# Dilated attention with V as weights: outputs feature by token, shares spread by 0/1 products, halves of y_b inside the attention groups

## The chip, the cores and the metric

One core of a Trainium2 chip runs the whole layer. The metric is the device time of one execution in microseconds (us). Five engines run in parallel, each through its own queue in program order: PE (TensorE: weight loads and matmuls), DVE (VectorE), ACT (ScalarE), POOL (GpSimd) and SP, which here issues most DMA transfers. A matmul keeps one operand, the weights, in the array and streams the other, the moving operand, through it.

## What is computed

A decoder layer on x of 2048 tokens by 1024 features, all in float32:

```python
proj = x @ w_in[l] + b_in[l]
q, k, v, g_attn, u_lru, g_lru, gate_logits = jnp.split(proj, SPLIT_POINTS, axis=-1)
...
for g, (window, dilation) in enumerate(DILATION_GROUPS):   # (128,1), (512,4), (2048,16)
    o_g, lse_g = dilated_band_attention(q[:, :, g], k[:, :, g], v[:, :, g], window, dilation)
wts = jax.nn.softmax(jnp.stack(lses, axis=0), axis=0)
attn = jnp.sum(wts[..., None] * jnp.stack(outs, axis=0), axis=0)
attn = attn.reshape(B, S, ATTN_OUT_WIDTH).astype(dt) * jax.nn.silu(g_attn)
y_a = attn @ w_attn_proj[l]
...
y_b = (h * jax.nn.silu(g_lru)) @ w_lru_proj[l]
merged = gates[:, :, 0] * y_a + gates[:, :, 1] * y_b
out = merged @ w_out[l] + b_out[l]
x = layer_norm(DEEPNORM_ALPHA * x + out, ln_gain[l], ln_bias[l])
```

Each of the three groups has 8 heads of 64 features. In a group, the tokens of one residue modulo the dilation form a sequence, cut into blocks of 128 queries; a block sees its own 128 keys and, where there is one, the block before.

## The kernel before

The kernel runs in four stretches. **Stage A** (to about 1456 us of the trace) is the input projection: 72 feature tiles by 4 token chunks of 512, by one Strassen step, with every product as three fp32r products of split halves (high by high, high by low, low by high); rotary q and k, V, the LRU branch and the gates hang on it and end in DRAM scratch. Its order is a list of ticks with due times and a budget per engine. **Stage B** (1456 to 1720 us) is attention. **Stage C** (1720 to 1905 us) is y_b = (gated h) times w_lru_proj, with the combination of the three groups beside it. **Stage D** (from 1905 us) is y_a, the merge, w_out and the layer norm.

Stage B goes over 12 units; a unit is a pair of heads of one group (order of the groups: 0, 2, 1, four times), with 16 query blocks; step `j` handles two blocks. `scores(j)` gives for both heads of the pair q times k: the heads lie in partitions 0 to 63 and 64 to 127, so that a product has 64 rows, and the two heads' products stand next to each other in the queue and go to different PSUM banks. q and k are split in halves (`q_split`, `k_split` on ACT and POOL), three products a head. Group 2 has no block before; there 256 columns are computed all the same and half of them not used. `weigh(m)` adds the mask and takes the minimum (the negated maximum) in one DVE operation, then ACT takes exp; the minimum lies beside the outputs in tile `osb`. `turn_p(j)` turns the shares p by transposes, in halves of 64 queries (64 rows each, banks t0 and t1); `copy_p` brings them to `ptb` in SBUF. `values(j)` takes `ptb` as weights (128 keys by 128 queries) and streams V with a column of ones, 65 columns a head, in plain float32; DVE copies the result to `osb`, and POOL issues the store to `o_scr`. Steps are interleaved by hand: two steps of scores, turns of earlier ones, then the values of two steps, so that four blocks make one round.

Stage C has 32 jobs of 24 products (`yb_job`: chunk c, feature tile f; 128 rows, 512 columns, fp32r), the weights `WL` split once for all chunks. `combine` loads three groups' outputs token by feature, takes exp of the differences of the minima, scales on POOL by a broadcast, adds, turns the result by four transposes (`ctp`) and gates it into `at_scr`.

Of the kernel before, what the change touches and what calls it, by code (L numbers as in the profile page):

```python
# [8 lines left out]
F32 = mybir.dt.float32  # L9
# [22 lines left out]
def hybrid_block_kernel(ctx: ExitStack, tc: tile.TileContext, a: dict, out: bass.AP):  # L32
# [10 lines left out]
    o_scr = [[dram.tile([S, 132], F32, name=f"o_scr{g}{hp}") for hp in range(HP)] for g in range(3)]  # L43
# [28 lines left out]
    bn = cst.tile([P, 72], F32, name="bn")  # L72
    lr = cst.tile([P, 8, 8], F32, name="lr")
# [23 lines left out]
    X = ctx.enter_context(tc.tile_pool(name="X", bufs=1))  # L97

    def big(slot, shape, dt, name):
        return (Y if slot[0] == "Y" else Z if slot[0] == "Z" else X).tile(shape, dt, name=name, tag=slot)  # L100

# [40 lines left out]
    LAST_SLOTS = [*range(15, 19), *range(29, 32), *range(28, 18, -1), *range(14, -1, -1)]  # L142
# [254 lines left out]
    def silu_chain(y, sgn, f, c):  # L397
# [3 lines left out]
        act.activation(y, y, AF.Identity, scale=0.5 * sgn, bias=bh[:, f:f + 1])  # L401
# [370 lines left out]
    QSLOT, KSLOT = ("X3", "X1", "Y0"), ("X4", "Y3")  # L772
    VSLOT = {(0, 0): "X5", (2, 0): "Y1", (1, 0): "Y2", (0, 1): "X5", (2, 1): "Y1", (1, 1): "Y2"}
    KR = {}

    units = {}
# [5 lines left out]
    def k_parts(u):  # L782

        g, hp = unit(u)
        src = qk_scr["k", 4 * g + hp].rearrange("(d h) s -> h d s", h=2)

        def part(h, hs):
            def fn():
                if h == 0 and u % 2 == 0:
                    KR["t"] = big(("X2", "X0")[u // 2 % 2], [P, 2, S], F32R, f"C{u}")  # L790
                if h == 0:
                    units[u] = [None, None, KR["t"][:, u % 2]]
                sp.dma_start(flat(units[u][2][hs]), src[h])
            return fn

        return [part(0, lo_), part(1, up_)]

    def k_split(u, x):

        if x == 0:  # L800
            units[u][1] = big(KSLOT[u % 2], [P, S], F32R, f"B{u}")

        def piece(t):
            if unit(u)[0] == 2:
                return t.rearrange("p (c x) -> p c x", c=4)[:, :, 256 * x:256 * x + 256]
            return t[:, 1024 * x:1024 * x + 1024]

        lo, hi = piece(units[u][2]), piece(units[u][1])
        pool.tensor_copy(hi, flat(lo))
        pool.tensor_tensor(out=lo, in0=flat(lo), in1=flat(hi), op=ALU.subtract)  # L810

    def q_parts(u):

        g, hp = unit(u)
        q = qk_scr["q", 4 * g + hp].rearrange("(d h) s -> h d s", h=2)

        def part(h):
            def fn():
                if h == 0:
                    units[u][0] = big(QSLOT[u % 3], [P, 2, S], F32R, f"A{u}")  # L820
                sp.dma_start(flat(units[u][0][(lo_, up_)[h], 1]), q[h])
            return fn

        return [part(h) for h in range(2)]

    def q_split(u, i):

        hi, lo = (units[u][0][:, x, i * CH:(i + 1) * CH] for x in range(2))
        act.activation(hi, flat(lo), AF.Copy)
        pool.tensor_tensor(out=lo, in0=flat(lo), in1=flat(hi), op=ALU.subtract)  # L830

    VT = {}

    def v_parts(g, j):
        src = v_scr[g][j]

        def part(i):
            def fn():
                if i == 0:
                    VT[g, j] = big(VSLOT[g, j], [P, 16, 260], F32, f"V{g}{j}")  # L840
                V = VT[g, j]
                if g == 0:
                    sp.dma_start(V[:, 4 * i:4 * i + 4], src[i * CH:(i + 1) * CH].rearrange("(n p) f -> p n f", p=P))
                elif g == 1:
                    sp.dma_start(V[:, 4 * i:4 * i + 4], src[i * CH:(i + 1) * CH].rearrange("(j r) f -> j r f", r=4))
                else:
                    sp.dma_start(V[:, 4 * i:4 * i + 4], src.rearrange("(i r) f -> i r f", r=16)[:, 4 * i:4 * i + 4])
            return fn

        return [part(i) for i in range(4)]  # L850


    def biases():
        dve.tensor_scalar(out=bh, in0=b72, scalar1=0.5, scalar2=None, op0=ALU.mult)
        dve.tensor_scalar(out=bn, in0=b72, scalar1=-1.0, scalar2=None, op0=ALU.mult)

# [45 lines left out]
    firstv = v_parts(0, 0)  # L902
    R0 = {}

    def first_raw(n):
        for i in K4:
            r = R0[n, i] = take(f"r{n}{i}", F32)
            src = qk_scr[n, 0].rearrange("(d h) s -> h d s", h=2)
            for h, hs in enumerate((lo_, up_)):
                sp.dma_start(r[hs], src[h][:, i * CH:(i + 1) * CH])  # L910

    def first_tiles():
        KR["t"] = big("X2", [P, 2, S], F32R, "C0")
        units[0] = [None, None, KR["t"][:, 0]]

    def first_split(n, i):
        if n == "q" and i == 0:
            units[0][0] = big(QSLOT[0], [P, 2, S], F32R, "A0")
        if n == "k" and i == 0:
            units[0][1] = big(KSLOT[0], [P, S], F32R, "B0")  # L920
        A, B, C = units[0]
        cs = slice(i * CH, (i + 1) * CH)
# [12 lines left out]
    for T, (s, j) in enumerate(where):  # L935
# [10 lines left out]
        if s == NQ - 1:  # L946
            for fn in begin.get(j, ()):
                fn()
            for x in split0.get(j, ()):
                first_split(*x)  # L950
# [585 lines left out]
```

## Time and profile before

| | |
|---|---|
| time, median of 3 runs | 2181.79 us (2179.45 to 2183.22) |
| the profiled execution | 2181.37 us; span of its trace 2179.5 us |
| stage A, 0 to 1456 us | PE busy 1449.9 us |
| stage B, 1456 to 1720 us | PE busy 260.0, DVE 193.5, ACT 221.9, POOL 169.1 us |
| stage C, 1720 to 1905 us | PE busy 183.0, DVE 144.1, ACT 33.6, POOL 99.0 us |
| stage D, 1905 to 2179.5 us | PE busy 262.3, DVE 188.1, ACT 34.9, POOL 46.5 us |
| granted TensorE clock | 0.999 of full speed |

Busy time of PE is the union of its matmuls, each from its start to its modelled end; since one starts long before the one ahead has ended, a busy PE says that work stood in the array, not how fast it went. What one matmul costs in a stream is read from a run of them: the run's length by their number. A product in plain float32 stands twice in the trace (600 `values` products in the program, 1200 matmuls in the trace); an fp32r product and a transpose stand once.

### The profile page before, as it was taken

How to read it: one execution, taken by the hardware profiler on the slowest of the kernel's cores; microseconds unless marked ns; L12 is line 12 of the kernel's file. 1: busy time of each engine (PE TensorE's matmuls, PEld its weight loads, DVE VectorE, ACT ScalarE, POOL GpSimd, SP SyncE). 2: the span in 40 equal slices, each digit the busy share in tenths (PEclk: the TensorE clock that was granted, in tenths of full speed). 3: DMA queues.
4: the chain of work that ended last, by engine and by line, in shares of the span. 5: the costliest groups of instructions: out<-in, count | busy, mean ns of one | idle time of the engine just before them, and what ended most of it. 6: DMA issues, size and time to landing. Idle time of an engine off the chain costs nothing.

```text
span 2179.5 us, 35322 instructions
## 1 busy us (share of the span) xinstructions
PE 2155.2 (99%) x12025; PEld 1803.7 (83%) x12025; DVE 1703.7 (78%) x3209; ACT 1220.3 (56%) x2206; POOL 774.1 (36%) x603
## 2 busy tenths in 40 slices
PE   9999999999999999999999999999999999999998
PEld 7888888888888888888888888879999878888786
DVE  8787987998899767687688798667777588867667
ACT  5456456557556666767767877758888511221100
POOL 2544554555555011021021021027666356622120
PEclk9999999999999999999999999999999999999999
DMA  7876976977877775676575675698774688864431
GB/s 227 255 220 195 264 228 204 265 224 235 256 216 230 242 221 172 184 220 175 184 221 165 198 230 176 189 292 242 208 196 130 191 282 281 263 203 149 156 116 68
DMA packets 257187, 456.05 MB, mean 209 GB/s; under 512 B 58752, under 2 KB 89504, under 8 KB 254192
## 3 DMA queue, kind: packets, MB, share of 16 engines
q1 hardware_dynamic: 237984, 412.70, 60.4%
q0 software_dynamic: 14128, 32.19, 7.1%
q10 hardware_dynamic: 4896, 8.92, 1.1%
q8 instruction: 95, 1.56, 0.3%
q14 instruction: 84, 0.69, 0.1%
HBM read 290.07 MB, written 163.64 MB: 208 GB/s over the span
## 4 chain that ended last, share of the span: by engine, by line
PE 55%; DMA 4%; issue 4%; DVE 2%; ACT 1%; POOL 1%; SPq 0%; ACTq 0%; POOLq 0%; DVEq 0%
PE q L627 32%; PE o L1063 5%; PE yb L1301 2%; PE yb L1299 2%; PE yb L1300 2%; PE s L1003 2%; PE pt L1032 2%; DMA V<-v_scr 1%; PE z L1413 1%; PE z L1412 1%; PE z L1411 1%; POOL me L1382 1%; PE g L488 1%; DMA atr<-at_scr 1%; ACT p L1018 1%
## 5 line engine op out<-in xcount | busy, mean ns | idle before, releaser
L627 PE MATMUL q<-xT,hS 128*128 128x512 f32 x1632 | 504.7, 390 | 0.0
L627 PE MATMUL q<-xT,l 128*128 128x512 f32 x1088 | 423.7, 389 | 0.1
L627 PE MATMUL q<-xB,hA 128*128 128x512 f32 x1344 | 417.4, 392 | 0.0
L627 PE MATMUL q<-xB,l 128*128 128x512 f32 x944 | 367.8, 390 | 1.7 <-DMA l<-wl_scr 1.7
L627 PEld LDWEIGHTS q<-xT,hS 128*128 128x128 f32 x1632 | 304.8, 188 | 64.3 <-issue 1.8
L627 PEld LDWEIGHTS q<-xB,hA 128*128 128x128 f32 x1344 | 250.4, 188 | 56.6 <-issue 5.5
L627 PEld LDWEIGHTS q<-xT,l 128*128 128x128 f32 x1088 | 204.2, 188 | 43.3 <-DMA l<-wl_scr 0.5
L233 POOL TENSOR_TENSOR sw<-sw,sin 128x512 f32<-128x512 f32 x96 | 155.8, 1628 | 167.8 <-ACT sw L322 71.3
L627 PEld LDWEIGHTS q<-xB,l 128*128 128x128 f32 x944 | 177.3, 188 | 39.4 <-DMA l<-wl_scr 2.1
L233 POOL TENSOR_TENSOR y<-y,h 128x512 f32<-128x512 f32 x28 | 39.2, 1399 | 384.1 <-DVE h L529 368.0
L627 PE MATMUL q<-xB,hS 128*128 128x512 f32 x544 | 168.8, 391 | 1.1 <-DVE v L233 1.1
L627 PE MATMUL q<-xT,hA 128*128 128x512 f32 x544 | 167.9, 390 | 0.0
L277 ACT ACTIVATE hA<-wA 128x512 fp32r<-128x512 f32 x220 | 138.6, 636 | 31.8 <-DVE l L233 11.6
L1018 ACT ACTIVATE p<-p,osb 128x256 f32<-128x256 f32 (+1 forms) x384 | 145.3, 451 | 18.9 <-DVE osb L1016 18.3
L277 ACT ACTIVATE hS<-S 128x512 fp32r<-128x512 f32 x170 | 108.4, 638 | 64.4 <-DVE S L233 46.1
L1063 PE MATMUL o<-V,ptb 128*128 128x65 f32 x1200 | 144.4, 277 | 0.0
L1063 PEld LDWEIGHTS o<-V,ptb 128*128 128x128 f32 x1200 | 137.7, 192 | 3.3
L233 POOL TENSOR_TENSOR l<-wA,hA 128x512 fp32r<-128x512 f32 x68 | 110.3, 1622 | 84.7 <-ACT hA L277 51.2
L1016 DVE CUSTOM_DVE_ANT_0 p<-s,mask 128x256 f32<-128x256 f32 (+1 forms) x384 | 116.9, 361 | 24.2 <-PE s L1003 16.9
L627 PEld LDWEIGHTS q<-xB,hS 128*128 128x128 f32 x544 | 101.2, 188 | 22.6 <-issue 2.2
L627 PEld LDWEIGHTS q<-xT,hA 128*128 128x128 f32 x544 | 101.8, 188 | 21.8 <-ACT hA L277 0.4
L233 DVE TENSOR_TENSOR S<-S,wA 128x512 f32<-128x512 f32 x102 | 98.2, 963 | 11.6 <-DMA wA<-in_w_in_dram 8.1
(207 smaller groups left out, 4645.8 us busy)
## 6 DMA issues: line engine op xcount, KB each, us to landing
wA<-in_w_in_dram SPq DMA_DIRECT2D x220, 256.0 KB, 5.1
wl_scr<-l SPq DMA_DIRECT2D x102, 512.0 KB, 5.3
l<-wl_scr SPq DMA_DIRECT2D x102, 512.0 KB, 4.4
wS<-in_w_in_dram SPq DMA_DIRECT2D x102, 256.0 KB, 4.3
wS<-in_w_in_dram POOLq DMA_DIRECT2D x68, 256.0 KB, 6.9
mg_scr<-y SPq DMA_DIRECT2D x59, 256.0 KB, 5.1
o_scr<-osb POOLq DMA_DIRECT2D x48, 264.0 KB, 5.4
oc<-o_scr SPq DMA_DIRECT2D x48, 264.0 KB, 4.9
```

Source lines behind the costliest of these rows:

```text
L233: eng.tensor_tensor(out=out, in0=in0, in1=in1, op=op)
L277: act.activation(heads(h), heads(r, False), AF.Copy)
L488: pe.matmul(g, gw[hs, l], x[hs], start=(n == 0), stop=(n == 2))
L627: pe.matmul(bank, w[:, ks], x[:, kk, xx], start=(first and i == 0), stop=(last and i == 11))
L1003: pe.matmul(bank[h][:, b, (0 if g == 2 and n else lo):256], A[hs, x, n * P:(n + 1) * P], k, start=(i == 0), stop=(i == 2))
L1016: dve.tensor_tensor_reduce(out=p[:, h, lo:256], in0=bank[h][:, m % 2, lo:256], in1=mask[:, lo:256], scale=1.0, scalar=3e38, op0=ALU.add, o ...
L1018: act.activation(p[:, h, lo:256], p[:, h, lo:256], AF.Exp, scale=-1.0, bias=mm)
L1032: pe.transpose(pt[e][:, b, 2 * h + x, :], p[hs, h, x * P:(x + 1) * P], ident[hs, hs])
L1063: pe.matmul(o[:, b, h * 65:h * 65 + 65], ptb[:, b, 2 * h + x, :], V[:, kb, vo + h * 65:vo + h * 65 + 65], start=(x == lo // P), stop=(x == 1))
L1299: pe.matmul(yb, WL[f][:, 0, k], xx[:, 0], start=(k == 0), stop=False)
L1300: pe.matmul(yb, WL[f][:, 0, k], xx[:, 1], start=False, stop=False)
L1301: pe.matmul(yb, WL[f][:, 1, k], xx[:, 0], start=False, stop=(k == 7))
```

## The change

Stages A and D keep their instructions and order, but for the last unit of stage A, where the first unit's q and k are no longer split, and for where w_attn_proj and w_out are split. Stages B and C become one stretch of 49 groups (`G`) of four blocks each and a rest:

- `scores`: one product a head in plain float32 in place of three in fp32r; nothing is split; group 2 computes 128 columns.
- `weigh`: minima go to a tile of the unit, `ML`, and the exp sums its row by `accum_out` (the column of ones in V is gone).
- `values`: V is the weights (128 keys by 64 features), `ptb` streams (128 columns), and the two heads of the pair write partitions 0 to 63 and 64 to 127 of one bank, alternating. The output is feature by token and stays in SBUF (`OT`), so that `o_scr`, its stores and loads and the `ctp` transposes go. One copy of 512 columns a group replaces two of 260.
- The shares of the groups are computed on 32 partitions: `turn_ml` turns minima and sums, `load_ml` brings them in three stages through DRAM, `weights` works on them (mostly POOL), and `spread` brings the result to 64 partitions a head by a product with a 0/1 matrix (512 columns, fp32r, 48 in all); DVE multiplies from PSUM, POOL adds and gates.
- `y_b` in halves: a group G from 4 on ends with half a job (12 products), in 42 groups (two groups rest, after jobs 7 and 15). The other 22 halves follow the attention. `WL` holds two jobs, so that each job loads and splits its weights anew (POOL inside the groups, ACT and DVE after them). The factor 0.5 moves into the gate (`silu_chain`).

```diff
-        act.activation(y, y, AF.Identity, scale=0.5 * sgn, bias=bh[:, f:f + 1])
+        if f < FT_U:
+            act.activation(y, y, AF.Identity, scale=0.5 * sgn, bias=bh[:, f:f + 1])
+        else:
+            act.activation(y, y, AF.Identity, scale=0.25 * sgn, bias=bq[:, f - FT_GL:f - FT_GL + 1])
...
     def scores(j):
...
-        A, hi, low = units[u]
+        q, k_ = AT_X["qk", u % 2][:, 0], AT_X["qk", u % 2][:, 1]
...
-            for i, (x, B) in enumerate(((0, hi), (0, low), (1, hi))):
-                for h, hs in enumerate((lo_, up_)):
-                    if g == 2:
-                        k = B[hs].rearrange("p (c r i) -> p r c i", c=4, r=16)[:, max(n - 1, 0):n + 1]
...
-                    pe.matmul(bank[h][:, b, (0 if g == 2 and n else lo):256], A[hs, x, n * P:(n + 1) * P], k,
-                              start=(i == 0), stop=(i == 2))
+            for h, hs in enumerate((lo_, up_)):
+                if g == 2:
+                    k = k_[hs].rearrange("p (c r i) -> p r c i", c=4, r=16)[:, n]
...
+                pe.matmul(bank[h][:, b, lo:256], q[hs, n * P:(n + 1) * P], k, start=True, stop=True)
             st["s", 2 * j + b] = (bank, lo)
...
+            ML[u] = at_p.tile([P, P], F32, tag="ml", name=f"ml{u}", bufs=2)
+            pool.memset(ML[u][:, 64:P], 0.0)
+        p = PT[:, m % 8]
...
-            act.activation(p[:, h, lo:256], p[:, h, lo:256], AF.Exp, scale=-1.0, bias=mm)
+            act.activation(p[:, h, lo:256], p[:, h, lo:256], AF.Exp, scale=-1.0, bias=mm, accum_out=ll)
...
-        on_act = e == 0 or j % 4 == 0
+        on_act = e == 0
...
-    def values(j):
...
-        o = aps.tile([P, 2, 130], F32, tag="o", name=f"o{j}", bufs=2)
...
-                    pe.matmul(o[:, b, h * 65:h * 65 + 65], ptb[:, b, 2 * h + x, :],
-                              V[:, kb, vo + h * 65:vo + h * 65 + 65], start=(x == lo // P), stop=(x == 1))
...
-        dve.tensor_copy(osb[:, b:b + 2, 0:130], o)
...
-            later(2, lambda: pool.dma_start(dst, osb))
...
+    def values(js):
+        o = aps.tile([P, 4, P], F32, tag="o", name=f"o{js[0]}", bufs=1)
...
+                    for h, hs in enumerate((lo_, up_)):
+                        pe.matmul(o[hs, 2 * i + b, :], V[:, kb, 64 * h:64 * h + 64], ptb[:, b, 2 * h + x, :],
+                                  start=(x == lo // P), stop=(x == 1))
...
+            dve.tensor_copy(dst, o[:, i:i + m])
...
+    def spread(hp, c, g, tag):
...
+        w = cur["ps"].tile([P, CH], F32, tag=tag, name=f"w{hp}{c}{g}", bufs=cur["wb"])
+        pe.matmul(w, sel[:, g], st["wh", hp, c], start=True, stop=True)
+        tt(dve, os[g], os[g], w, ALU.mult)
...
+        def join():
+            tt(pool, os[0], os[0], os[g], ALU.add)
+            if g == 1:
+                tt(pool, os[0], os[0], st.pop(("ga", hp, c)), ALU.mult)
+                later(1, lambda: sp.dma_start(at_scr[hp * P:(hp + 1) * P, cs], os[0]))
...
+    def split_wl(n):
+        t = WL[:, n % 2]
+        inside = cur["ps"] is aps
...
+            if inside:
+                pool.tensor_copy(t[:, 0, ks], r)
+            else:
+                act.activation(t[:, 0, ks], r, AF.Copy)
+            tt(pool if inside else dve, t[:, 1, ks], r, flat(t[:, 0, ks]), ALU.subtract)
...
+    def yb_part(n, k):
...
+        w, x = WL[:, n % 2], hx(8 * c + k)
+        pe.matmul(YB["t"], w[:, 0, k], x[:, 0], start=(k == 0), stop=False)
+        pe.matmul(YB["t"], w[:, 0, k], x[:, 1], start=False, stop=False)
+        pe.matmul(YB["t"], w[:, 1, k], x[:, 0], start=False, stop=(k == 7))
...
+    for G in range(NG + 1):
+        run(late)
+        if G < NG:
+            if G:
+                turn_p(2 * G - 2)
+                copy_p(2 * G - 2, 0)
+                copy_p(2 * G - 2, 1)
+            scores(2 * G)
+            weigh(4 * G)
+            weigh(4 * G + 1)
+            scores(2 * G + 1)
+            if G:
+                turn_p(2 * G - 1)
+                copy_p(2 * G - 1, 0)
+                copy_p(2 * G - 1, 1)
+            weigh(4 * G + 2)
+            weigh(4 * G + 3)
+            if G:
+                values([j for j in (2 * G - 3, 2 * G - 2) if j >= 0])
+        else:
...
+        y = G >= GY and G not in rests and (G < NG or len(halves) % 2)
+        if y:
+            n, hf = divmod(halves[0], 2)
+            yb_part(n, 4 * hf)
+            yb_part(n, 4 * hf + 1)
+        for i, x in enumerate(spreads.pop(G, ())):
+            spread(*x, f"t{i}")
+        if G % 4 == 0 and G:
+            turn_ml(G // 4 - 1)
+        if y:
+            yb_part(n, 4 * hf + 2)
+            yb_part(n, 4 * hf + 3)
+            if hf:
+                yb_done(n)
+            yb_care(halves.pop(0))
+            if hf and n in (7, 15):
+                rests.add(G + 1)
+        now["n"] += 1
...
+    for t in halves:
+        n, hf = divmod(t, 2)
+        run(late)
+        for fn in rest.pop(t - r0, ()):
+            fn()
+        yb_part(n, 4 * hf)
+        yb_part(n, 4 * hf + 1)
+        for x in more.pop(t - r0, ()):
+            spread(*x, "z")
+        yb_part(n, 4 * hf + 2)
```

On PE, the scores of one query block with 256 columns. Before, three products for each of the two heads (`s` is the bank of a head, `B` and `C` the halves of k, `A` q):

```order
L1003 MATMUL s_14698<-B_14013,A_13938 128x256
L1003 MATMUL s_14699<-B_14013,A_13938 128x256
L1003 MATMUL s_14698<-C_13831,A_13938 128x256
L1003 MATMUL s_14699<-C_13831,A_13938 128x256
L1003 MATMUL s_14698<-B_14013,A_13938 128x256
L1003 MATMUL s_14699<-B_14013,A_13938 128x256
```

Now the scores of three such blocks stand in as many rows (`qk` holds q and k unsplit; each row is two matmuls on the engine):

```order
L974 MATMUL s_15102<-qk_14098 128x256
L974 MATMUL s_15103<-qk_14098 128x256
L974 MATMUL s_15118<-qk_14098 128x256
L974 MATMUL s_15119<-qk_14098 128x256
L974 MATMUL s_15118<-qk_14098 128x256
L974 MATMUL s_15119<-qk_14098 128x256
```

Two rows a block are left of six. The second place is the end of a round on PE, in a unit of group 2. Before, the values of two steps end it and the next turns follow (`pt` are the transposed shares, `ptb` their copy):

```order
L1032 MATMUL pt_14737<-ident,p_14665 128x64
L1032 MATMUL pt_14738<-ident,p_14665 128x64
L1063 MATMUL o_14760<-V_13978,ptb_14649 128x65 x4
L1063 MATMUL o_14766<-V_13978,ptb_14687 128x65 x4
L1032 MATMUL pt_14775<-ident,p_14713 128x64
L1032 MATMUL pt_14776<-ident,p_14713 128x64
```

Now, at the end of a group with full blocks, the values write 64 partitions each and half a y_b job stands between them and the next turns; once in four groups the transpose of the minima (`mlt`) stands in its middle:

```order
L1034 MATMUL o_15153<-ptb_15015,V 64x128 x8
L1034 MATMUL o_15153<-ptb_15083,V 64x128 x8
L1197 MATMUL yb_15174<-hx_13946,wl 128x512
L1198 MATMUL yb_15174<-hx_13946,wl 128x512
L1199 MATMUL yb_15174<-hx_13946,wl 128x512
L1197 MATMUL yb_15174<-hx_13946,wl 128x512
L1198 MATMUL yb_15174<-hx_13946,wl 128x512
L1199 MATMUL yb_15174<-hx_13946,wl 128x512
L1055 MATMUL mlt_15181<-ident,ml_14704 128x128
L1197 MATMUL yb_15174<-hx_13946,wl 128x512
L1198 MATMUL yb_15174<-hx_13946,wl 128x512
```

The twelve fp32r products that stood in stage C now stand between the values and the turns of the next group.

More of the change, by code (lines that the diff above doesn't have):

```diff
@@ L1343, in hybrid_block_kernel @@
             prep_wo(*wo.pop(0))
[L1344 to L1349 removed]
+        now["n"] += 1
+    for k in sorted(rest):
+        for fn in rest[k]:
+            fn()
+    assert not more
+    for _ in range(2):
         run(late)
[L1351 removed]
         now["n"] += 1
@@ L1452, in hybrid_block_kernel @@
     split_m(TT[0], slice(6, 8))
-    run(late)
-    assert not late
+    while late:
+        run(late)
+        now["n"] += 1
     load_xr(TT[0])
```

652 lines of the change are left out of this document (323 added, 329 removed).

## The prediction

> **What bounds the kernel now.** I read the busy times by stretch first, then what PE waited for in stages B and C (engine, line, releaser: total us, times, longest).
>
> ```profile
> PE 2155.2 (99%) x12025; PEld 1803.7 (83%) x12025; DVE 1703.7 (78%) x3209; ACT 1220.3 (56%) x2206; POOL 774.1 (36%) x603
> ```
> ```profile
> 1456.00:1720.00 264.00, 260.02 (x3552) 250.18 (x3552) 193.45 (x941) 221.90 (x572) 169.11 (x145) 1.00 0.71 198
> 1720.00:1905.00 185.00, 182.99 (x836) 150.42 (x836) 144.09 (x376) 33.63 (x71) 99.00 (x81) 1.00 0.83 268
> ```
> ```profile
> PE pt L1032 <- ACT ptb L1045: 3.0, 9, 0.8
> PE ctp L1235 <- issue: 1.1, 1, 1.1
> PE yb L1299 <- ACT wl L1093: 0.6, 1, 0.6
> ```
>
> The columns of the middle two rows are length, then busy time (instructions) of PE, weight loads, DVE, ACT, POOL, then clock, DMA share and GB/s. Stages B and C last 264 + 185 = 449 us, and PE stands idle for some 6 us of them. So PE's queue sets the time, and the sum is made of its products at their pace in a stream. In the timeline a row gives start, length, shape and count; a round of four full blocks (group 0) looks so:
>
> ```profile
> 1538.75 3.79 PE L1063 MATMUL o<-V,ptb 128*128 128x65 f32 x32
> 1542.47 0.71 PE L1032 MATMUL pt<-ident,p 64*128 64x64 f32 x16
> ...
> 1544.48 0.65 PE L1032 MATMUL pt<-ident,p 64*128 64x64 f32 x16
> 1545.06 3.79 PE L1063 MATMUL o<-V,ptb 128*128 128x65 f32 x32
> ```
> ```profile
> 1549.25 1.50 PE s L1003 x24
> ...
> 1555.95 1.93 PE o L1063 x16
> 1558.27 1.50 PE s L1003 x21
> ```
>
> The second fence is the chain of waits, where a row's length runs to the next piece. Values: 3.72 us (1538.75 to 1542.47) by 32 is 0.116 us a matmul; scores: 1.50 by 24 is 0.0625, or 0.125 for the two heads' 256 columns that run at once; turns: 0.52 to 0.58 us by 16. A round takes 1545.06 - 1538.75 = 6.3 us, 3.7 of it values.
>
> **The price of a plain float32 matmul.** The trace has it with 65 columns only; here are durations (min/median/max ns) of weight loads (PEld) and matmuls by tile:
>
> ```profile
> L1063 PEld LDWEIGHTS o<-V,ptb x1200: 186/192/192, 1462.8 to 1720.0; 128*128 128x128 f32 x172
> L1063 PE MATMUL o<-V,ptb x1200: 275/275/325, 1462.8 to 1720.0; 128*128 128x65 f32 x172
> L1032 PEld LDWEIGHTS pt<-ident,p x1200: 134/138/142, 1458.7 to 1716.3; 64*128 64x128 f32 x172
> L1032 PE MATMUL pt<-ident,p x1200: 213/222/275, 1458.7 to 1716.3; 64*128 64x64 f32 x172
> L1235 PE MATMUL ctp<-ident,oc x64: 270/272/301, 1762.5 to 1904.8; 128*128 128x128 f32 x64
> L1003 PE MATMUL s<-B,A x768: 269/279/381, 1456.0 to 1708.6; 64*128 64x256 f32 x168, 64*128 64x128 f32 x24
> L1300 PE MATMUL yb<-h,wl x256: 387/389/397, 1720.4 to 1904.0; 128*128 128x512 f32 x128
> ```
>
> From 256 to 512 columns fp32r grows by 110 ns, 0.43 ns a column, over a fixed part of 169. The float32 transposes (`ctp`, 128 columns: 272; `pt`, 64: 222) then stream at 0.8 ns a column. `o` is 106 ns over the fixed part with 65 columns: either 1.6 ns a column, or 0.8 and a wait of some 53 ns for weights, whose load is as much longer than that of the transposes (192 against 138). I take the second: the first matmul of a burst shows the same 50 ns once more (325), as a weight load not yet hidden would. Then a stream of narrow float32 matmuls is held by its weight loads, at 0.116 us, and up to 128 columns cost about that; 256 columns cost 213 ns and a gap of 15 as in the scores' pairs, 0.228.
>
> **The change, part by part.** PE, in us:
>
> - *Scores*. 108 blocks have 256 columns (15 + 12 + 0 of 16 in the three groups, times 4), 84 have 128. Now each takes two matmuls a head, the heads at once on their row halves as before: 108 x 2 x 0.228 + 84 x 2 x 0.12 = 49 + 20 = 69. Before: 48 rounds x 1.5, less where the trace has fewer, 70. Nothing gained: the narrower group 2 pays for the wider price.
> - *Values*. Before 1200 x 0.116 = 139. The 1200 remain, with 64 weight columns and 128 streamed, at 0.12. If the heads run at once on their column halves: 72; if one after the other: 144. No run of it stands in the trace; the nearest rows are the pairs on row halves (`s`, 0.125 us for two), so I take 72, and keep 144. Gain **67**.
> - *Turns*: the same 1200.
> - *y_b*: 768 products at 0.227 (starts in the rows below) as before, 174; 16 groups of four `ctp` transposes go (1762.28 to 1762.86 is 0.58, less 0.227: 0.35 each, 5.6), 48 spreads at 0.227 (10.9) and 12 turns of the minima (1.3) come. Loss **7**.
> - *Changes of shape*: into 64 rows, into 64 columns, back to the full array. Into the row halves cost 0.31 from start to start, 0.08 over a product (786.83 to 787.14). A group has one more than a round: 48 x 0.1, loss **5**.
>
> ```profile
> 1762.28 0.39 PE L1301 MATMUL yb<-h,wl 128*128 128x512 f32 x1
> 1762.51 0.60 PE L1235 MATMUL ctp<-ident,oc 128*128 128x128 f32 x4
> 1762.86 0.47 PE L1299 MATMUL yb<-h,wl 128*128 128x512 f32 x1
> ...
> 786.83 0.39 PE L627 MATMUL q<-xT,l 128*128 128x512 f32 x1
> 787.14 0.50 PE L488 MATMUL g<-vh,gw 64*128 64x512 f32 x2
> ```
>
> PE's work falls by 67 - 7 - 5 = **55** us. What the Trainium skill says on the open price: *TensorEngine Tiling (Array Packing)*, Key Properties, has tiles "execute LdWeights and Matmul in parallel" for column halves as for row halves, and that changing the tiling mode drains the engine. By the first the values cost 72 rather than 144, by the second every change of shape pays; the trace agrees for row halves (0.125 for two) and for the drain (0.08), and shows no column halves.
>
> **The cover.** A full group on PE: scores 1.9, turns 1.1, values 1.9, y_b 2.7, changes 0.3: 7.9 us; in group 2 about 5.4. Beside it:
>
> ```profile
> 1569.52 1.70 ACT L1018 ACTIVATE p<-p,osb 128x256 f32<-128x256 f32 x4
> ...
> 1571.64 0.58 ACT L1045 ACTIVATE ptb<-pt 128x512 f32<-128x512 f32 x1
> ```
> ```profile
> 1704.71 0.41 DVE L1016 CUSTOM_DVE_ANT_0 p<-s,mask 128x256 f32<-128x256 f32 x1
> 1705.05 0.08 DVE L1016 DVE_READ_ACCUMULATOR2_ANT osb<- 128x1 f32 x1
> 1705.05 0.42 DVE L1016 CUSTOM_DVE_ANT_0 p<-s,mask 128x256 f32<-128x256 f32 x1
> ```
> ```profile
> 1564.63 1.05 POOL L809 CAST B<-C 128x1024 fp32r<-128x1024 f32 x1
> ...
> 1573.37 1.29 POOL L830 TENSOR_TENSOR A<-A 128x512 fp32r<-128x512 f32 x1
> ```
> ```profile
> L1213 ACT ACTIVATE cE<-cE 128x24 f32<-128x24 f32 x16 | 3.6, 223 | 132.7 <-DVE cE L1212 132.7
> ```
> ```profile
> L1094 DVE SCALAR_TENSOR_TENSOR wl<-wlr,wl 128x512 fp32r<-128x512 f32 x13 | 10.6, 856 | 1.7 <-ACT wl L1093 1.7
> L1091 DVE TENSOR_TENSOR wo<-wor,wo 128x512 fp32r<-128x512 f32 x8 | 9.3, 1171 | 0.0
> ```
> ```profile
> C<-k_scr SPq DMA_DIRECT2D x20, 512.0 KB, 12.3
> V<-v_scr SPq DMA_DIRECT2D x18, 520.0 KB, 10.0
> ```
>
> ACT: 8 exps x 0.42 and 2 copies x 0.55, 4.5. Summing by `accum_out` isn't in the trace; between nothing and 0.22 (the exp of 24 elements, `cE`), and I take DVE's read of its own accumulator, 0.08, which is the same kind of step: 5.1, at most 6.3. DVE: 8 x 0.35, 2 x 0.6 for copies, 0.7 for the outputs, 0.35 for y_b: 5.1, with two spreads 6.5; in group 2, where the reductions are half as wide, about 5 with spreads. POOL splits a job's weights in 2 x (0.5 + 1.3) = 3.6 each two groups, and adds and gates at 1.3. All lie under PE, but the margins in group 2 are half a microsecond. That the outputs are written with a stride in groups 1 and 2 I cost at nothing: DVE has the room, at most 0.4 a group.
>
> Waits that are new: the spreads use the banks of the turns, so the next group's first turn waits for DVE's two multiplications, which run beside six y_b products (1.4 us by 1.4 us: nothing, or some tenths where DVE is late); a half of y_b waits for POOL's split, and behind it in PE's queue stand the turns and scores, so whatever POOL is late by, all of it is late. Q, k and V of a unit are asked for a unit ahead, 22 to 32 us, and land in 10 to 12; those of the first unit are asked for six products (16 us) before the end of stage A, and cost at most the 2 or 3 us by which four transfers run over. The order of SP's queue has them ahead of the weights of y_b, which have two groups.
>
> What shows: six groups without y_b, where ACT is as long as PE (3, with the first transfers); the end of attention, where group 48 has no y_b to cover minimum, exp, turn, copy and values (4); POOL splitting four tiles of h (7 us) behind a job's weights after jobs 7 and 15, two groups ahead of need (2 x 2); the rest of 22 halves (60 us), where DVE has 42 splits at 0.8 to 1.2 and 23 reads of PSUM at 0.7, some 55 us (4). Together **15**.
>
> Sum: 2181.4 (the profiled execution: span and 1.9 around it; it lies 0.4 under the median) - 55 + 15 = 2141; by the ends of `accum_out` 2138 to 2150. I forecast **2141**.
>
> **Rivals.** (1) *The column halves don't overlap*: each head's stream waits for the other's. The values then cost 144, PE's work rises by 17, and the time is 2141 + 72 = **2213**. It decides as soon as a pair costs over (72 + 40)/600 = 0.19 us in place of 0.12. For it: no row shows column halves, and both heads now read the same V block and write one bank. Against it: the array does run row halves at once. (2) *Float32 streams at 1.6 ns a column*: 128 columns cost 0.22, 256 0.43. Scores 108 x 0.88 + 84 x 0.44 = 132, values 600 x 0.22 = 132: **2264**. Against it is the 325. (3) *Transfers or another engine set the pace*. q, k, V, the weights anew and h are some 70 MB over 330 us, 212 GB/s, where stage B moved 198 at a share of 0.71 and stage C 268 at 0.83; the load sits in the first half of each unit. Two us late in each of 12 units is 24: **2165**, and ACT at its upper price in group 2 comes to the same.
>
> **How the numbers follow.** (A measurement of this kernel tells about 0.2%, 4 us, from no change.) Forecast 0.58 (2120 to 2157), rival 1 0.15, rival 2 0.06, rival 3 0.16 (2157 to 2185), 0.05 for less than 2120. The range holds the forecast, rival 3 and most of rival 1: **2120 to 2216**. Under 2177.5 lie the forecast, the small case and most of rival 3: faster 0.75; within 0.2% 0.04; slower, rivals 1 and 2 with a little of 3, 0.21.
>
> **What would show it.** The run of 32 value matmuls of a full group (3.72 now): 1.9 us if the halves overlap, 3.8 if not, 3.6 if float32 streams slowly. Eight score products 1.8 us, or 3.5. A full group 7.9 us from turn to turn. Waits of PE's turns for ACT, or of y_b for POOL, of over 15 us together would be rival 3, and so would units whose first scores wait for q and k. The forecast is wrong if stages B and C together are not near 409 us.

## The result and the profile after

The changed kernel takes 2154.87 us (median of 4 runs, 2152.37 to 2158.05) against 2182.51 us for the kernel before on the same chip: a ratio of 0.987, with a 95% interval of 0.9843 to 0.9898. The forecast was 2141 us: faster, as forecast, but by 27.6 us and not by 41. The profiled execution took 2158.05 us, the longest of the four; its span is 2156.1 us.

The page of the changed kernel has, in its first part, busy time, share of the span and instructions of each engine:

```profile
PE 2109.7 (98%) x11637; PEld 1728.5 (80%) x11637; DVE 1658.8 (77%) x2958; ACT 1211.2 (56%) x2482; POOL 746.8 (35%) x661
```

In the view by windows, the stretch from the first scores to the first product of y_a (what were stages B and C), then stage D, in the columns of the prediction's windows:

```profile
1450.70:1877.00 426.30, 397.55 (x3998) 323.91 (x3998) 294.77 (x1068) 245.91 (x921) 240.38 (x283) 0.98 0.79 212
1877.00:2156.10 279.10, 264.70 (x1153) 216.60 (x1151) 192.05 (x319) 38.02 (x59) 45.89 (x30) 0.98 0.42 139
```

The first stretch was 449 us, with PE idle for 6; now it is 426.3, with PE idle for 426.30 - 397.55 = 28.7. Before, the granted clock was full there; now it is 0.98. It stood at half in four places:

```profile
1471.50:1478.30 6.80, 5.62 (x57) 5.54 (x59) 2.55 (x17) 3.90 (x17) 6.56 (x9) 0.50 1.12 263
1597.80:1601.20 3.40, 3.40 (x26) 2.48 (x26) 1.21 (x2) 0.60 (x1) 3.24 (x5) 0.51 1.03 176
1730.90:1737.70 6.80, 4.83 (x49) 4.38 (x50) 3.44 (x18) 5.45 (x19) 5.85 (x9) 0.50 0.63 193
1836.70:1840.10 3.40, 3.40 (x9) 2.62 (x9) 1.81 (x4) 0.63 (x1) 0.00 (x0) 0.51 0.89 316
```

In these four PE worked for 5.62 + 3.40 + 4.83 + 3.40 = 17.2 us at half clock, which is 8.6 us of work lost. So the stretch divides into 28.7 us idle, 8.6 lost at half clock, and 426.3 - 28.7 - 8.6 = 389 us of products. Before, the products were 443 us. **PE's work fell by 54 us; idle time and half clock gave back 31.**

What the products cost is read from a full group, in the timeline:

```profile
1631.19 0.71 PE L1002 MATMUL pt<-ident,pt 64*128 64x64 f32 x16
1631.74 1.95 PE L974 MATMUL s<-qk 64*128 64x256 f32 x16
1633.52 0.66 PE L1002 MATMUL pt<-ident,pt 64*128 64x64 f32 x16
1634.11 1.97 PE L1034 MATMUL o<-ptb,V 128*64 128x128 f32 x32
...
1638.95 0.71 PE L1002 MATMUL pt<-ident,pt 64*128 64x64 f32 x16
```

The group takes 1638.95 - 1631.19 = 7.8 us. The eight score products take 1633.52 - 1631.74 = 1.8 us, and the row of the 32 value matmuls 1.97 us, where it had 3.79. So the column halves do run at once, and float32 does not stream slowly: the first two rivals fell at this row. What PE waited for, by line and releaser (total us, times, longest), shows the rest (`pt` are the turns, `w` the spreads, `wh` the loaded shares, `wl` the weights of y_b, `mlt` the turns of the minima):

```profile
PE pt L1002 <- ACT ptb L1015: 8.2, 4, 6.3
PE w L1131 <- DMA wh<-w_scr: 5.8, 4, 3.3
PE yb L1197 <- ACT wl L1165: 5.3, 2, 4.2
...
PE s L974 <- DMA qk<-k_scr: 2.7, 2, 2.0
...
PE mlt L1055 <- DVE o L236: 1.7, 3, 0.6
```

Before, the turns waited 3.0 us for ACT, y_b 0.6 for its weights, and the other lines had no counterpart. The longest single wait, followed back through all engines in the timeline (an SPq row runs from the first issue of a group to its last):

```profile
1721.35 0.68 DVE L1050 COPY o<-o 128x512 f32<-128x512 f32 x1
...
1722.29 7.24 SPq L1074 DMA_DIRECT2D mt<-ml_scr  x8
...
1729.53 0.37 DVE L236 TENSOR_TENSOR wm<-mt 32x128 f32<-32x128 f32 x1 [7.49 <-DMA mt<-ml_scr]
...
1730.23 0.67 DVE L1017 COPY ptb<-pt 128x512 f32<-128x512 f32 x1
...
1732.87 1.12 PE L1002 MATMUL pt<-ident,pt 64*128 64x64 f32 x16 [6.35 <-ACT ptb L1015]
```

The wait names ACT, but ACT had nothing to do. DVE stood at the minimum over the three groups (`top`, the row at 1729.53), whose inputs SP was still asking for, piece by piece, until 1729.5. Behind it in DVE's queue stood the copies and the mask-and-minimum operations of the next blocks, so that ACT got no exps and PE no turns. SP itself had stood 2.1 us until the store of the minima had landed, and two of its eight loads stood 1.7 us for the q and k asked for before them. Half clock began in this wait, at 1730.9 us.

### The profile page after: what moved, and what is told of

Same layout as the page of the kernel before. It is cut to its first block, busy times and chain, and to the rows that moved or that the text cites. A ratio compares the mean times of both kernels' runs of the same rounds, so it can differ in the third digit from the quotient of the medians.

```text
span 2156.1 us, 34641 instructions
## 1 busy us (share of the span) xinstructions
PE 2109.7 (98%) x11637; PEld 1728.5 (80%) x11637; DVE 1658.8 (77%) x2958; ACT 1211.2 (56%) x2482; POOL 746.8 (35%) x661
## 4 chain that ended last, share of the span: by engine, by line
PE 82%; DMA 8%; issue 3%; POOL 2%; DVE 2%; SPq 1%; ACT 1%; ACTq 0%; POOLq 0%; DVEq 0%
PE q L633 64%; PE o L1034 2%; PE s L974 2%; PE yb L1197 2%; DMA wh<-w_scr 1%; PE pt L1002 1%; PE z L1498 1%; PE z L1496 1%; PE z L1497 1%; PE yb L1198 1%; PE yb L1199 1%; DMA atr<-at_scr 1%; POOL me L1467 1%; PE vtp L366 1%; DMA wor<-in_w_out_dram 1%
## 5 line engine op out<-in xcount | busy, mean ns | idle before, releaser
L988 ACT ACTIVATE pt<-pt,ml 128x256 f32<-128x256 f32 (+1 forms) x384 | 172.1, 451 | 27.8 <-DVE ml L986 27.8
L986 DVE CUSTOM_DVE_ANT_0 pt<-s,mask 128x256 f32<-128x256 f32 (+1 forms) x384 | 117.0, 361 | 8.5 <-PE s L974 6.6
L324 ACT ACTIVATE sw<-y 64x512 f32<-64x512 f32 x96 | 60.6, 631 | 82.7 <-DVE y L577 79.5
L1498 PE MATMUL z<-wo,ms 128*128 128x512 f32 x256 | 100.4, 392 | 2.6 <-DVE ms L1483 2.6
```

Of the source, the lines that this page charges most:

```text
L324: act.activation(flat(sw)[lo_], flat(rw)[up_], AF.Copy, scale=scale)
L986: dve.tensor_tensor_reduce(out=p[:, h, lo:256], in0=bank[h][:, m % 2, lo:256], in1=mask[:, lo:256], scale=1.0, scalar=3e38, op0=ALU.add, o ...
L988: act.activation(p[:, h, lo:256], p[:, h, lo:256], AF.Exp, scale=-1.0, bias=mm, accum_out=ll)
L1498: pe.matmul(z, ml[:, k], w[:, 0, hs], start=False, stop=(k == 7))
```

## The experiments

The theory: the products cost what the prediction said, and the missing 14 us are waits which the chain of the shares (its loads and stores through DRAM, its operations on POOL, DVE and ACT) makes in queues that work in order, with half clock behind them. Rivals: the waits come of transfers and of denser work as such; or ACT with its sums has become the pace. Times of one kernel spread over 3 to 10 us from run to run, so moves of a few us are read from the trace. The table has the stretch from the first scores to y_a in the profiled run of each, divided as above (half clock by the trace's records of the granted clock):

| run | median us | ratio to before, 95% | stretch | PE idle | lost at half clock | products |
|---|---|---|---|---|---|---|
| changed kernel | 2154.9 | 0.984 to 0.990 | 426.3 | 28.7 | 8.6 | 389.0 |
| e1, again | 2154.4 | 0.986 to 0.990 | 421.9 | 26.9 | 5.3 | 389.7 |
| e2, shares later | 2153.5 | 0.985 to 0.989 | 415.5 | 20.8 | 5.1 | 389.6 |
| e3, store by POOL | 2155.9 | 0.986 to 0.990 | 425.4 | 27.6 | 8.7 | 389.1 |
| e4, q and k first | 2152.3 | 0.985 to 0.988 | 421.0 | 26.1 | 4.7 | 390.2 |
| e5, heads apart | 2185.2 | 1.000 to 1.003 | 454.1 | 15.3 | 4.1 | 434.7 |
| e6, no shares | 2115.0 | 0.966 to 0.972 | 383.9 | 9.2 | 1.7 | 373.0 |
| e7, y_b after | 2246.5 | 1.025 to 1.033 | 514.0 | 87.2 | 31.2 | 395.6 |
| e8, apart, no shares | 2156.6 | 0.984 to 0.990 | 427.5 | 6.5 | 1.7 | 419.3 |
| e9, three moves | 2148.4 | 0.981 to 0.987 | 415.7 | 21.3 | 4.8 | 389.6 |
| e10, and the rest | 2147.1 | 0.980 to 0.986 | 411.3 | 18.4 | 4.4 | 388.5 |
| e11, shares first | 2142.8 | 0.980 to 0.983 | 406.0 | 16.3 | 0 | 389.7 |
| e12, no sums | 2157.4 | 0.986 to 0.989 | 426.4 | 30.0 | 8.3 | 388.1 |

The last column is the first finding: wherever the products are the same ones, they cost 388 to 390 us, and the two columns before it hold all that differs. (In e7, where most groups are broken by waits, they come to 396.)

**e1, the changed kernel again.**

> The changed kernel once more, unaltered, so that the next three stand beside it on one chip. All theories: 2155 us, PE waits of about 28 us between 1450 and 1877 us, and the granted clock at half in five stretches of 3.4 or 6.8 us.

2154.42 us. The waits came again, at the same lines, 26.9 us in all; half clock came in three places, where the first profile had four and a fifth in stage D. So the waits belong to the kernel, and how much half clock follows them varies.

**e2, the shares one group later.**

```diff
-        for i, g in enumerate((1, 2, 2, 3, 4)):
+        for i, g in enumerate((1, 3, 3, 4, 5)):
...
-            at_group(e + (5, 5, 8, 9)[c], lambda hp=hp, c=c: load_wh(hp, c))
+            at_group(e + (6, 6, 9, 10)[c], lambda hp=hp, c=c: load_wh(hp, c))
...
-            spreads.setdefault(e + 6 + i // 2, []).append((hp, c, g))
+            spreads.setdefault(e + 7 + i // 2, []).append((hp, c, g))
```

> The steps of the shares from the minimum over the groups on, and the spreads, one group later. Theory (the missing time is waits in queues that work in order: an instruction that needs the chain of the shares stops all that stands behind it): the wait of the turns for ACT at 1732.9 us (6.4 us; DVE stood 7.5 us before the minimum) goes, and with it the half clock from 1730.9 to 1737.7 us (3.4 us of work): 8 to 10 us faster than the changed kernel, 2145 to 2147. Rival (the waits and the half clock come from the denser products themselves, whatever the order): the wait turns up elsewhere, within 3 us of 2155.

The view of PE's waits:

```profile
PE yb L1197 <- ACT wl L1165: 7.0, 3, 3.3
PE mlt L1055 <- DVE o L236: 3.4, 6, 0.6
...
PE s L974 <- DMA qk<-k_scr: 2.8, 1, 2.8
...
PE w L1131 <- DMA wh<-w_scr: 2.0, 1, 2.0
PE pt L1002 <- ACT ptb L1015: 1.9, 3, 0.9
```

The wait of the turns fell from 8.2 to 1.9 us with the half clock behind it, and that of the spreads from 5.8 to 2.0 (4.8 in e1). The same move stands in e9 to e11: there the longest wait of the turns for ACT is 0.9 to 1.3 us, where it is 5.4 to 6.6 in the first profile, e1, e3, e4 and e12, which don't have it. So the mechanism is shown. In turn y_b waited more for its weights (5.3 to 7.0) and the turns of the minima for DVE (1.7 to 3.4). The stretch was 11 us shorter than that of the changed kernel and 6 shorter than that of e1; but the profiled run was the fastest of its four, and the median fell by 1 us only, within the spread of the runs. The 8 to 10 us of the theory did not come: in time it was as the rival said, part of the wait turned up elsewhere.

**e3, the shares' stores issued by POOL.**

```diff
-                sp.dma_start(w_scr[hp].rearrange("(y h) (p i) -> h p y i", h=2, i=P)[h],
+                pool.dma_start(w_scr[hp].rearrange("(y h) (p i) -> h p y i", h=2, i=P)[h],
```

> The stores of the shares to DRAM are issued by POOL, which computes them, and not by SP. Theory: at 1836 us the wait of y_b for ACT (4.3 us, and half clock for 3.4 us after it) comes from SP standing 8.6 us before this store with the weights of y_b behind it; it goes: 4 to 6 us faster than the changed kernel, 2149 to 2151. Rival (y_b waits because ACT and DVE need longer to split its weights than PE takes for a half): no gain, 2155, and the wait stays at 4 us.

```profile
PE w L1131 <- DMA wh<-w_scr: 8.2, 3, 4.1
...
PE w L1131 <- DVE o L236: 2.6, 1, 2.6
...
PE yb L1197 <- ACT wl L1165: 1.7, 2, 1.0
```

The wait of y_b for its weights went from 5.3 to 1.7 us, so it did come from SP standing before that store. But the spreads now waited 8.2 + 2.6 us for the shares themselves, where it had been 5.8 + 0.8: the time stayed at 2155.9. Taking the block out of one queue doesn't bring the shares sooner, and the 4 to 6 us of the theory did not come.

**e4, q and k of the second unit first.**

```diff
+    for fn in qk_parts(1):
+        at_group(0, fn)
     at_group(0, selectors)
...
-    for fn in qk_parts(1):
-        at_group(1, fn)
```

> q and k of the second unit are asked for ahead of the tiles of h, in group 0. Theory: the scores' waits for them (0.7 and 2.0 us at 1470 to 1473 us) and the half clock from 1471.5 to 1478.3 us (3.4 us of work) go: 4 to 6 us faster than the changed kernel, 2149 to 2151. Rival (the transfers of the start are too many together, whatever their order): the wait moves to y_b's first product for h, no gain, 2153 to 2157.

The wait of the scores (2.7 us) is gone from the view, with the half clock there. y_b then waited for POOL's splits by 0.5 and 0.9 us. The median fell by 2.1 us under e1's, within the spread of the runs, where 4 to 6 were expected; the half clock at this place was only 3.4 us long in e1, so there was less to win.

**e5, the heads of a pair apart.** All value products of one head, then all of the other:

```diff
-                        pe.matmul(o[hs, 2 * i + b, :], V[:, kb, 64 * h:64 * h + 64], ptb[:, b, 2 * h + x, :],
-                                  start=(x == lo // P), stop=(x == 1))
+                        mm[h].append((o[hs, 2 * i + b, :], V[:, kb, 64 * h:64 * h + 64], ptb[:, b, 2 * h + x, :],
+                                      x == lo // P, x == 1))
...
+        for y, w, x, start, stop in mm[0] + mm[1]:
+            pe.matmul(y, w, x, start=start, stop=stop)
```

> The values of a group in another order: first all products of the one head, then all of the other, so that no two neighbours in PE's queue stand on different column halves. Theory (the gain of the values, 67 us, comes from neighbours that run at once): 32 products take 3.7 to 3.8 us in place of 1.9, 600 pairs at 0.113 more are 68 us: 2215 to 2225. Rival (64 weight columns are cheaper by themselves, in loading or in streaming): 32 products stay under 2.5 us, at most 2175.

```profile
1665.70 3.33 PE L1041 MATMUL o<-ptb,V 128*64 128x128 f32 x32
1668.96 0.50 PE L1199 MATMUL yb<-hx,wl 128*128 128x512 f32 x1
```
```profile
L1041 PEld LDWEIGHTS o<-ptb,V x1200: 132/137/230, 1458.4 to 1832.5; 128*64 128x64 f32 x172
```
```profile
1452.00:1906.10 454.10, 438.79 (x3998) 367.20 (x3998) 298.58 (x1068) 246.17 (x921) 240.01 (x283) 0.99 0.74 199
```

(The first fence is the timeline, the second the view by tile with the weight loads' shortest, median and longest ns, the third the stretch.)

The order alone costs 31 us (2185.2 against 2154.4): running at once is real. But both expectations missed the size: 32 products take 1668.96 - 1665.70 = 3.3 us, not 3.7 to 3.8, since a float32 matmul with 64 weight columns takes 0.10 us by itself, not 0.116. Its weights load in 137 ns, where 128 columns took 192; but 128 streamed columns at the 0.8 ns that the prediction read from the transposes are 0.10 us too, and no run tells the two apart. PE's products rose by 434.7 - 389.0 = 46 us, and the time by 31, because idle time fell from 28.7 to 454.10 - 438.79 = 15.3 us and what half clock cost from 8.6 to 4.1. The wait of the spreads for the shares is 0.9 us here (5.8 before the edit): with longer groups they arrive in time.

**e6, no shares.** What computes, stores, loads and spreads the shares is left out (the steps, `load_ml`, `load_wh`, `turn_ml`, and in `spread`:)

```diff
-        pe.matmul(w, sel[:, g], st["wh", hp, c], start=True, stop=True)
-        tt(dve, os[g], os[g], w, ALU.mult)
```

> The shares of the groups are left out: no turn of the minima, no loads of them, no work on 32 partitions, no spreads and no multiplication by them (the outputs of the three groups are added as they are); all else stays, the adding and gating too. Both theories take away 48 spreads and 12 turns, 12 us of products. Theory (the missing 14 us are waits that the chain of the shares makes in the queues of SP, DVE and POOL, and half clock after them): another 15 to 25 us, 2118 to 2128. Rival (the waits come of transfers and of attention with y_b itself): 12 to 15 us in all, 2140 to 2143.

```profile
1452.80:1836.70 383.90, 374.67 (x3937) 309.55 (x3937) 261.94 (x1008) 240.83 (x905) 210.48 (x223) 1.00 0.85 232
```

2115.0 us, 39.9 under the changed kernel; the theory said at least 2118, the rival 2140 or more. The chain costs 16 us of products (389.0 - 373.0, where the prediction had 12) and, of idle time and half clock, (28.7 + 8.6) - (9.2 + 1.7) = 26 us; beside e1 it is 21. This run takes away work of DVE and POOL too, so it doesn't tell their work from the order of their queues; e9 to e11 do. The largest wait that stays is that for q and k of the second unit, 3.7 us.

**e7, y_b after attention.**

```diff
-    GY = 4
+    GY = 99
...
-    r0 = halves[0]
-    assert r0 == 42, r0
+    r0 = 42
```

> All 64 halves of y_b after attention, none in its groups. Theory (the halves cover ACT and DVE, which need 5.1 to 6.5 us a group, where PE alone would need 5.2 in groups 0 and 1 and 2.6 in group 2): 16 groups of group 2 wait 2.5 us each and 24 groups with spreads about 1 us each, with half clock behind some of it: 40 to 85 us slower than the changed kernel, 2195 to 2240. Rival (attention flows by itself, and where the halves stand makes no difference): 2150 to 2162.

```profile
PE pt L1002 <- DVE o L236: 19.1, 30, 1.3
PE w L1131 <- DMA wh<-w_scr: 14.9, 3, 5.6
PE pt L1002 <- ACT ptb L1015: 13.6, 20, 2.5
PE pt L1002 <- ACT mls L1057: 10.7, 11, 1.5
```

92 us slower than e1, more than the 85 at which the expectation ended. PE stands idle for 87 us, and half clock costs 31, a term that the expectation had named and not priced. The waits are the ones which the halves cover: DVE's multiplications in the banks of the turns, ACT's copies, the shares' loads. That y_b stands inside the groups is what makes the attention part of this change worth its products.

**e8, both e5 and e6.**

> Both edits at once: the values of the two heads one after the other, and no shares. Beside the run without shares alone (2115 us) it shows what the order of the values is worth where the chain of the shares makes no waits; with the chain it was worth 31 us, though its products took 0.085 us more a pair, 51 us. Theory (of what the halves save, some 20 us are given back as waits for the chain of the shares): 2115 + 45 to 51, 2160 to 2166. Rival (the products cost less than their rows say, or the waits come from the shorter groups alone): 2115 + 28 to 35, 2143 to 2150.

```profile
1451.50:1879.00 427.50, 421.00 (x3938) 356.59 (x3938) 262.88 (x1008) 241.07 (x905) 210.59 (x223) 1.00 0.76 208
```

2156.6 us, 41.6 over e6: between the two expectations and nearer to the theory. The products differ by 419.3 - 373.0 = 46 us, as with the shares in place, and idle time with half clock by 3 us instead of 18 (13 beside e1). So with the chain in place some 15 of the halves' 46 us are given back, without it 3 to 5.

**e9, e10 and e11: better orders.** e9 joins e2 and e4 and stores the gated outputs a group later:

```diff
-                later(1, lambda: sp.dma_start(at_scr[hp * P:(hp + 1) * P, cs], os[0]))
+                later(2, lambda: sp.dma_start(at_scr[hp * P:(hp + 1) * P, cs], os[0]))
```

e10 adds, in the rest of y_b:

```diff
-        if hf:
-            if n + 2 < 32:
-                load_wl(n + 2)
+        if hf == (cur["ps"] is aps) and n + 2 < 32:
+            load_wl(n + 2)
+        if hf:
...
-    rest = {1: [lambda: step(3, 0)], 4: [lambda: step(3, 1)], 5: [lambda: step(3, 2)], 6: [lambda: step(3, 3)],
-            7: [lambda: step(3, 4)], 9: [lambda: load_wh(3, 3), lambda: load_wh(3, 0)],
+    rest = {2: [lambda: step(3, 0)], 5: [lambda: step(3, 1)], 6: [lambda: step(3, 2)], 7: [lambda: step(3, 3)],
+            10: [lambda: step(3, 4)], 11: [lambda: load_wh(3, 3), lambda: load_wh(3, 0)],
...
-    more = {(11, 12, 15, 16)[i]: [(3, c, g) for g in (0, 2, 1)] for i, c in enumerate(CO)}
+    more = {(13, 14, 16, 17)[i]: [(3, c, g) for g in (0, 2, 1)] for i, c in enumerate(CO)}
```

e11 puts the loads of the shares at the head of their groups, ahead of q, k, V and h:

```diff
-            at_group(e + (6, 6, 9, 10)[c], lambda hp=hp, c=c: load_wh(hp, c))
+            todo.setdefault(e + (6, 6, 9, 10)[c], []).insert(c % 2 if c < 2 else 0, lambda hp=hp, c=c: load_wh(hp, c))
```

> Three moves together inside attention: the steps of the shares one group later, q and k of the second unit ahead of the tiles of h, and the stores of the gated outputs one group later, so that SP does not stand before POOL's product with loads behind it. Theory: no wait of over 1 us is left between 1451 us and the end of attention but the one of 1.2 us for the last outputs, and no half clock there; those of the rest of y_b stay: 2155 less 12 to 18, 2137 to 2143. Rival (each move hands the wait on to the next transfer, as the single moves did in part): 2148 to 2153.

> The three moves, and in the rest of y_b: its weights asked for half a job earlier, the last shares' loads behind the first weights, their store three halves later and their spreads two, one and one later. Theory: the waits of y_b for ACT (5 to 7 us together, and half clock) go as well: 6 to 9 us under the run with three moves, 2129 to 2136. Rival (the splits on ACT and DVE are what is late): the waits of y_b stay at 5 us or more, and the time within 3 us of the run with three moves.

> As the run with three moves and the rest reordered, and the loads of the shares for the spreads stand first in their groups, ahead of q, k, V and h. Theory: the wait of the spreads for them (4.2 us at 1603 us, with half clock for 6.8 us after it) shrinks to under 1.5 us: 4 to 7 us faster than that run, 2140 to 2143. Rival (the transfers there, h anew for a chunk with q, k and V, are too many for their order to help): the wait stays over 3 us, or another transfer is late, 2145 to 2150.

e9: 2148.4, a miss of its theory and at the edge of what its rival expected: the wait for the shares at 1601 us stayed, now 3.6 us long. e10 gives the stores of the last heads their old place again. 2147.1, a miss of its theory in time: the waits of y_b for ACT fell from 5.7 to 1.9 us, but that at 1603 us was 4.2, and stage D got longer. e11 came out as its theory said: that wait is gone, and the time is 2142.8 us, the lowest, a ratio of 0.9812 (0.9798 to 0.9826) whose interval lies clear of the changed kernel's, though not of e10's:

```profile
1452.00:1858.00 406.00, 389.66 (x3997) 316.64 (x3997) 297.83 (x1067) 245.34 (x920) 243.27 (x283) 1.00 0.82 220
1858.00:2143.20 285.20, 267.19 (x1153) 216.93 (x1151) 192.00 (x320) 38.61 (x60) 45.90 (x30) 0.98 0.42 141
```
```profile
PE pt L1002 <- ACT ptb L1015: 3.7, 5, 1.1
PE mlt L1055 <- DVE o L236: 3.4, 6, 0.6
PE yb L1197 <- ACT wl L1165: 1.7, 1, 1.7
...
PE w L1131 <- DMA wh<-w_scr: 1.2, 1, 1.2
```

The stretch has no half clock, and its 406 us lie 3 under the 409 that the prediction had for the changed kernel. Stage D, with 285 us, is 6 longer than in the changed kernel: its products wait 9.3 us there, against 5.5, for the splits of their inputs (`at`, `ms`) and for `gA`, and half clock is longer. The last split of w_out starts 37 us into it, where it was 30; whether they are the cause, and what a better order would give, is open.

**e12, no sums.** The exps without `accum_out` (ones stand for the sums):

```diff
-            act.activation(p[:, h, lo:256], p[:, h, lo:256], AF.Exp, scale=-1.0, bias=mm, accum_out=ll)
+            act.activation(p[:, h, lo:256], p[:, h, lo:256], AF.Exp, scale=-1.0, bias=mm)
```

> The changed kernel without accum_out in the exps: the sums of the rows are left out and ones stand in their place. ACT then needs 0.09 us less an exp, 0.7 us a group. Theory (ACT lies under PE, and where PE waits for ACT it was stopped by another queue): 2152 to 2156, as the changed kernel. Rival (ACT with its sums is as long as a group of group 2 and sets the pace there, 16 groups by 0.3 to 0.6 us): 2145 to 2150.

2157.4 us, as the changed kernel. ACT's sums cost nothing while ACT lies under PE, and the waits that name ACT stay (7.8 us for `ptb`, 8.2 before the edit). In the changed kernel's timeline:

```profile
1634.32 0.49 ACT L988 ACTIVATE pt<-pt,ml 128x256 f32<-128x256 f32 x1
1634.72 0.19 ACT L988 ACTIVATION_READ_ACCUMULATOR pt<-pt,ml 128x1 f32 x1
1634.81 0.50 ACT L988 ACTIVATE pt<-pt,ml 128x256 f32<-128x256 f32 x1
```

Exps follow each other by 0.49 us. Before, four took 1.70 us from the start of the first to the end of the last; one is 0.50 long, so they followed each other by 0.40. The read of the accumulator, 0.19 us, lies beside the end of one exp and the start of the next.

## Why the prediction was right, and where it fell short

- **Values, 67 us: right in mechanism and size.** 32 matmuls take 1.9 us, as it said. The price of rival 1 was too high (72 us more if the halves don't run at once; e5 shows 46 in products, 31 in time), because a float32 matmul with 64 weight columns takes 0.10 us alone; why is open (e5).
- **Scores, 0: right.** 1.8 us for 16 matmuls of 256 columns was expected and found, 0.22 a pair, so that float32 does not stream at 1.6 ns a column. That narrow float32 products are held by their weight loads, as the prediction chose to read the 65 columns, fits these rows and is not shown by a run of its own.
- **PE's work, -55: measured -54** (443 to 389). In it the spreads and what goes with them cost 16 us (e6), not 12.
- **`accum_out`, 0.08 us an exp: measured 0.09, and worth nothing in time** (e12).
- **"What shows", 15 us: the term that was mis-sized.** It is 31: idle time rose from 6.0 to 28.7 us, and 8.6 were lost at half clock, which the sum didn't have at all. So the stretch is 426 us and not near the 409 that the prediction named as its own sign. Of the four places that it priced, the first transfers (2.7 us), the end of attention (1.2) and the rest of y_b (6.4, of which 4.2 behind the store of the shares) made waits, POOL's splits of h none; the turns (8.2) and the spreads (7.3) waited beside them. The step that failed is the paragraph on the new waits. It named the banks of the turns and POOL's split, and took the shares' work as so many us of DVE and POOL under PE's cover. It didn't ask what each step of the chain waits for, and what stands behind it: the minimum in DVE's queue behind eight DMAs, the store in SP's queue behind POOL, with the weights of y_b behind it, the loads of the shares behind q, k, V and h. No operation of the chain is longer than 2 us, though POOL's nine for the last heads' shares take 6.5 us in a row (1825.0 to 1831.5) while SP stands before the store; each such wait stops a queue that PE needs within 5 to 8 us, a group's length. e6 puts the chain's waits and half clock at 21 to 26 us, and e2, e3 and e11 show three of the places one by one.
- **"Cost at most the 2 or 3 us", for q and k of the first units.** The first unit's cost nothing; the second's came behind eight tiles of h, waited for 2.7 us and were followed by half clock. "The order of SP's queue has them ahead of the weights of y_b" holds later, not here.
- **Outside the stretch** the sum had no change. Stage A ended 5.3 us sooner (before, it had waits of 1.67, 0.72 and 0.37 us that did not come again; the rest is not explained, and in e1 it is 3.6 us sooner), and stage D took 279.1 us in place of 274.7, with 2.7 us more of waits and 3.4 us at half clock, which cost 1.7 (276.7 in e1, without half clock). In the profiled execution the two all but cancel: 2181.4 - 54 + 31 - 5.3 + 4.5 = 2158.
- **Rival 3** said that other engines or transfers, two us late in each unit, would give 2165. The time lies between it and the forecast; that it still falls in the forecast's part of the range, which ended at 2157, is a matter of 2 us, and luck. Something other than PE did set the pace in places. It was not bandwidth: e6 and e11 move 232 and 220 GB/s in the stretch with fewer waits, the changed kernel 212. Most of it was the order of queues: e11, which takes no work away, brings idle time and half clock there from 37.3 us (32.2 in e1) to 16.3, and the time to 2142.8.

## What to carry to other kernels

When work moves under the cover of a full engine, its busy time can be the smaller part of the price (here 16 us of products against 21 to 26 of waits and half clock); follow each step that waits for DRAM or for a slow engine, and list what stands behind it in that queue. A chain with round trips wants its waiting instructions a group later than its data could come, and its loads ahead of bulk loads that nobody needs yet. A gain measured on one part (46 us of products) shows in the time only as far as the rest keeps up (31 us).

## What the runs showed of the hardware

- Half clock follows short waits. In all runs but e7, each of the 19 waits of PE of over 2.9 us after its first matmul was followed by half clock, for 3.4 or 6.8 us, which began in the wait or within 2 us after it; so were the four of e7. Of those between 1.3 and 2.8 us some were (1.93 us in e10) and some weren't (2.79 us in e2). The Trainium skill, *TensorE: Matmul & The Clock Gate*, Part 1, says the same of the steps (a free-running window of some 3.4 us), but has the clock fall after an idle window; here 2 us of idle time in the 3.4 us before it fell were enough at times (e10, at 1820.3 us), so the measurement decides. By these figures a wait of 3 us costs some 5 to 6 (an estimate: half of 3.4 to 6.8 us on top, less what PE stands idle of it).
- A float32 matmul of 128 columns with 64 weight columns takes 0.10 us alone (3.3 by 32) and 0.12 a pair on the two column halves, with both halves writing one PSUM bank: a factor of 1.7, not 2.
- The eight DMAs that bring the minima in, in small pieces, kept SP's queue for 7.24 us: 5.3 us are their issues, 0.65 to 0.73 each, where `gB` and the store of the minima beside them took 0.42 and 0.47; the rest is mostly waits for earlier transfers to land.
